# Neighbourhood attention in a fused encoder layer: a deeper pipeline, with the value products of two blocks in one run

## The chip, the cores and the metric

The kernel runs on one core of one Trainium2 chip. The metric is the device time of one execution in microseconds (us); lower is better. A core has five engines with a queue of instructions each, worked off in order: TensorE (PE, matrix products), VectorE (DVE), ScalarE (ACT), GpSimd (POOL) and SyncE (SP, here the issuer of nearly all transfers). They wait for one another through semaphores. Tiles live in SBUF, results of TensorE in PSUM.

## The reference

One layer of a hybrid encoder: 1024 tokens and 16 meta tokens of width 1024, all in float32.

```python
u = _rmsnorm(h, norm_g[l])
z = u @ w_in[l]
gq, gk, gv, r_f, r_b, g_gate, nq, nk, nv, n_gate = jnp.split(z, split_at, axis=-1)
...
s_loc = jnp.einsum('bchd,bicjhd->bhcij', q_r, k_g) * scale
...
s = jnp.concatenate([s_loc.reshape(B, H, W, wh * ww), s_meta], axis=-1)
p = jax.nn.softmax(s.astype(jnp.float32), axis=-1).astype(v.dtype)
...
o_na = o_na * jax.nn.silu(n_gate)
h = h + jnp.concatenate([o_gla, o_na], axis=-1) @ w_out[l]
```

Group B, which the change concerns, is neighbourhood attention on a 16 by 64 grid of tokens: 16 heads of 64, each query sees a window of 8 by 16 tokens and the 16 meta tokens.

## The kernel before, in words

Every dense product is made of three matmuls on a high and a low half (`mm3`, lines 413 to 416). The program has three stretches. **Start**, to about 60 us: x is loaded, split, and multiplied by the projection weights of the first pair of heads. **Neighbourhood attention**, to about 620 us: eight pairs of heads, one after the other. **Linear attention and output projection**, to the end.

The order on all engines is written out by one model of TensorE's time in the program, the class `Sched` (lines 70 to 136). A main generator yields what comes next: `("w", ns)` books TensorE time for the matmuls just issued, `("gap", ns)` lets at least that much time pass and fills it with steps of a second generator, the filler; `("to", x)` runs the filler up to a given amount of its own work; `("need", key)` runs it until a key is set. The filler is the dense work of what comes later: in the second stretch `fill_na` (L1348), which gives `dense_na(p)` (eight blocks of queries, keys and values in the natural layout, tiles `pn_na`) and `dense_gate(p)` (the gate, tiles `pz_na`) in turn. `S.defer(ns, fn)` has a function's instructions issued when the model's time has gone on by ns. So the model decides the order of each engine's queue, and the chip's semaphores decide the times.

For a pair, `attn(p)` (L775) waits until the pair's dense blocks are made. `k_prep` (L685) transposes the keys on TensorE (`kt`, L696) and builds the operands `K1` and `K2` on ACT, DVE and POOL; the queries come in pairs of blocks by `q_prep` (L725). After `ATTN_NS` of filler come nine steps. Step s does this:

- `transposes` (L822) of block s-1: six transposes of its probabilities (`pp<-ident,P`, L829), three for each of the two heads, copied out to `PT` by ACT for head 0 and DVE for head 1 (L833, L835). Each head first calls its normalisation (DVE, L813 to L818) if that has not been issued yet.
- `softmax` (L785) of block s: four score matmuls (`s`, L767 and L768), on DVE the bias, the maximum and its negation (L795, L798), on ACT the exponentials (L801, L802), and the normalisation deferred by `NORM_NS`.
- filler up to a share `PV_AT` of the step's part, then `pv` (L839) of block s-1: six products of values and `PT`, each in two passes, so twelve matmuls (`po`, L848). A stationary operand has 64 columns there, so the two heads fill the two halves of the array's columns. The third chunk of blocks 0 and 7 has only 16 rows (the meta tokens, `kvm`); the others take it from `VM`, which two transfers (`v_load`, L680) fill for each pair. After blocks 3 and 7 DVE multiplies by the gate (L858); after block 7 SP stores the pair's result (L860).
- filler for the rest of the step.

Step 8 holds no scores: the transposes of block 7, `LAST_NS` of filler, the value products of block 7. Only then does the next pair's `attn` start with its keys. PSUM has two banks each for the tags `pp` (transposes, keys), `ps` (scores) and `pd` (dense), one for `po` and one for `pt`; a softmax block keeps its two `P` tiles, of which there are four.

Beside this, in the start: `u_diag` (L374) builds on DVE a diagonal tile of the row scales `rs`, and `u_spread` (L378) multiplies it by ones on TensorE (`rb`, L381) to get the scales along the other axis. And for pairs 2 and 4 `wd_load` and `wd_prep` (L1010, L1017) fetch and split the decay weights, `WD_NS` after the pair's start: POOL clears rows, DVE makes the high part, ACT copies it, DVE subtracts twice.

Of the kernel before, what the change touches and what calls it, by code (L numbers as in the profile page):

```python
# [20 lines left out]
NPAIR = 8  # L21
# [15 lines left out]
LAST_NS = 3438.0  # L37
# [14 lines left out]
START_AT = {'load': {2: 9, 3: 15, 4: 18, 5: 21, 6: 27, 7: 34}, 'split': {2: 15, 3: 19, 4: 25, 5: 28, 6: 41, 7: 48}, 'rows': {0: 10, 1: 12, 2: 18, 3: 21, 4: 23, 5: 29, 6: 45, 7: 53}, 'rstd': {0: 15, 1: 16, 2: 21, 3: 27, 4: 35, 5: 43, 6: 48, 7: 55}, 'evac': {0: 18, 1: 21, 2: 27, 3: 35, 4: 43, 5: 52, 6: 59}, 'diag': {0: 31, 1: 42, 2: 42, 3: 55, 4: 55}, 'spread': {0: 46, 1: 63, 2: 57, 3: 59}}  # L52
BANKS = {2: ("po", 1), 3: ("pp", 2), 4: ("pp", 2), 5: ("pd", 2), 6: ("pd", 2), 7: ("po", 1)}
PUMP_AT = 5
LD_NS = (842.0, 589.0, 1838.0)
# [84 lines left out]
def kernel(  # L140
# [231 lines left out]
    dg = {}  # L372

    def u_diag(b):  # L374
        dg[b] = nap.tile([128, 128], F32, tag="dg", name=f"dg{b}", bufs=3)
        dve.tensor_scalar(dg[b], ident, rs[:, b : b + 1], None, OP.mult)

    def u_spread(b):  # L378

        ps = ps_tile("ps", f"rb{b}", 2)  # L380
        pe.matmul(ps[:, 0:128], ones, dg[b], start=True, stop=True)  # L381
        act.activation(rbc[:, b * 128 : b * 128 + 128], ps[:, 0:128], AF.Copy)
        S.adv(220)
# [154 lines left out]
    def dense_na(p):  # L538
# [50 lines left out]
        def at(pos):  # L589
            for kind, fn in (  # L590
                ("load", x_load), ("split", u_split), ("rows", x_rows), ("rstd", u_rstd),
                ("evac", lambda t: tile_evac(banks.pop(t), t)), ("diag", u_diag), ("spread", u_spread),
            ):
# [10 lines left out]
        for b in range(8):  # L604
# [26 lines left out]
            if p == 0 and b == 7:  # L631
                assert not banks
                for i in range(4):
                    if i:
                        S.defer(LD_NS[i - 1], lambda i=i: u_diag(4 + i))
                    S.defer(LS_NS[i], lambda i=i: u_spread(4 + i))
# [138 lines left out]
    def attn(p):  # L775
        yield ("need", ("nat", p))
        yield from k_prep(p)
        vload = v_load(p)
        yield ("gap", ATTN_NS)
        prev = None  # L780
        po = {}
        f0 = S.fill
        f1 = (p + 1) * (NAT_NS + GATE_NS) + (NAT_NS if p < 7 else GLA_NS - 9000.0)

        def softmax(u):  # L785
            n = span(u)[1]
            off = 144 if u == 0 else 0
            sm = nap.tile([128, 8], F32, tag="sm", name=f"sm{p}{u}", bufs=2)
            Ps, norms = [], []
            Q1["rest"]()  # L790
            for a in range(2):
                ps = qk(p, u, a)
                P = nap.tile([128, 432], F32, tag="P", name=f"P{p}{u}{a}", bufs=4)
                mx = sm[:, 4 + a : 5 + a]
                dve.tensor_tensor_reduce(  # L795
                    P[:, :n], ps[:, :n], wt[2 * p + a][:, off : off + n], 1.0, -3.0e38, OP.add, OP.max, mx
                )
                dve.tensor_scalar(mx, mx, -1.0, None, OP.mult)  # L798
                if n == 416:
                    loc, met = P.rearrange("p (b t) -> p b t", t=BLK)[:, :, 0:128], P[:, 128:144]  # L800
                    act.activation(loc, loc, AF.Exp, bias=mx, accum_out=sm[:, a : a + 1])  # L801
                    act.activation(P[:, 295:416:8], met, AF.Exp, bias=mx, accum_out=sm[:, 2 + a : 3 + a])  # L802
                else:
                    loc = P[:, :n]
                    act.activation(loc, loc, AF.Exp, bias=mx, accum_out=sm[:, a : a + 1])
                Ps.append((P, loc))

            if u % 2 == SILU_STEP:
                run_silu()

            def norm(a):
                s = sm[:, a : a + 1]
                r = sm[:, 6 + a : 7 + a]  # L813
                if n == 416:
                    dve.tensor_tensor(s, s, sm[:, 2 + a : 3 + a], OP.add)
                dve.reciprocal(r, s)
                loc = Ps[a][1]
                dve.tensor_scalar(loc, loc, r, None, OP.mult)  # L818

            return Ps, [S.defer(NORM_NS[0], lambda: norm(0)), S.defer(NORM_NS[1], lambda: norm(1))]  # L820

        def transposes(u, Ps, norm):  # L822
            ch = ((0, 128), (144, 128), (128, 16) if u in (0, 7) else (288, 128))
            PT = []
            for a in range(2):
                norm[a]()
                pp = ps_tile("pp", f"pp{p}{u}{a}", 2)
                for c, (c0, w) in enumerate(ch):
                    pe.transpose(pp[:w, c * 128 : c * 128 + 128], Ps[a][0][:, c0 : c0 + w], ident)  # L829
                t = nap.tile([128, 384], F32, tag="PT", name=f"PT{p}{u}{a}", bufs=4)  # L830
                for w, e0, e1 in ((128, 0, 256), (16, 256, 384)) if u in (0, 7) else ((128, 0, 384),):
                    if a == 0:
                        act.activation(t[:w, e0:e1], pp[:w, e0:e1], AF.Copy)  # L833
                    else:
                        dve.tensor_copy(t[:w, e0:e1], pp[:w, e0:e1])  # L835
                PT.append(t)
            return PT

        def pv(u, PT):  # L839
            u4 = u % 4  # L840
            if u4 == 0:
                po[0] = ps_tile("po", f"po{p}{u}", 1)
            b0 = span(u)[0]
            vals = [vnat[p][:, b0], vnat[p][:, b0 + 1], kvm[p][:, 128:256] if u in (0, 7) else VM[:, b0 + 2]]
            for c, V in enumerate(vals):
                w = V.shape[0]
                for a in range(2):
                    pe.matmul(  # L848
                        po[0][64 * a : 64 * a + 64, u4 * 128 : u4 * 128 + 128],
                        V[:, 64 * a : 64 * a + 64],  # L850
                        PT[a][:w, c * 128 : c * 128 + 128],
                        start=c == 0, stop=c == 2,
                    )
            if u4 == 3:
                finish(gate_rest)
                g = zt[("ng", p)]
                gv = g.rearrange("p (r i c) -> p i r c", r=16, i=8, c=8)[:, u - 3 : u + 1]
                dve.tensor_tensor(gv, po[0].rearrange("p (i r c) -> p i r c", i=4, r=16, c=8), gv, OP.mult)  # L858
                if u == 7:
                    sp.dma_start(o_scr[8 + p], g)  # L860

        for s in range(9):
            PT = None
            if prev is not None:
                PT = transposes(*prev)
                pu = prev[0]
                yield ("w", 654)
            if s < 8:
                prev = (s, *softmax(s))
# [10 lines left out]
            else:  # L880
                yield ("gap", LAST_NS)
            if PT is not None:
# [615 lines left out]
```

## Time and profile before

| | us |
|---|---|
| median of three runs | 1147.07 |
| the three runs | 1146.75, 1147.07, 1149.39 |
| the profiled execution | 1147.51 |
| its span, first to last instruction | 1145.7 |
| PE busy | 1122.2 |
| DVE, ACT, POOL busy | 769.9, 533.5, 300.7 |

The profile is of one execution. Its page gives each engine's busy time, the span in 40 slices, the chain of work that ended last, and groups of equal instructions (line, engine, operation, tile written, tile read, shape, count, busy time, mean duration, idle time before them). The trace behind it gives, for any stretch, the instructions in order of time and what each waited for. Matmuls are pipelined: a duration in the trace covers the whole way through the array, and the next one starts well before it ends, so what a matmul costs is read from the distance between starts.

### The profile page before, as it was taken

How to read it: one execution, taken by the hardware profiler on the slowest of the kernel's cores; microseconds unless marked ns; L12 is line 12 of the kernel's file. 1: busy time of each engine (PE TensorE's matmuls, PEld its weight loads, DVE VectorE, ACT ScalarE, POOL GpSimd, SP SyncE). 2: the span in 40 equal slices, each digit the busy share in tenths (PEclk: the TensorE clock that was granted, in tenths of full speed). 3: DMA queues.
4: the chain of work that ended last, by engine and by line, in shares of the span. 5: the costliest groups of instructions: out<-in, count | busy, mean ns of one | idle time of the engine just before them, and what ended most of it. 6: DMA issues, size and time to landing. Idle time of an engine off the chain costs nothing.

```text
span 1145.7 us, 18925 instructions
## 1 busy us (share of the span) xinstructions
PE 1122.2 (98%) x6739; PEld 976.7 (85%) x6739; DVE 769.9 (67%) x1963; ACT 533.5 (47%) x1379; POOL 300.7 (26%) x415
## 2 busy tenths in 40 slices
PE   8899999999999999999999999999999999999998
PEld 7789898888988889898889789889978978888886
DVE  6867777777677776777665775675486578656352
ACT  6756565664655656565454541542343254313120
POOL 4753535336253443634221101001101000000000
PEclk9999999999999999999999999999999999999999
DMA  8720402203030030401223513512612375314132
GB/s 259 225 75 2 128 2 73 63 2 128 1 109 27 10 120 1 128 2 32 76 57 102 165 28 84 153 36 79 170 42 66 93 206 166 120 42 130 50 115 102
DMA packets 74277, 99.34 MB, mean 87 GB/s; under 512 B 6532, under 2 KB 45188, under 8 KB 74184
## 3 DMA queue, kind: packets, MB, share of 16 engines
q1 hardware_dynamic: 69960, 89.76, 26.0%
q0 software_dynamic: 4224, 8.39, 2.5%
q8 instruction: 53, 0.87, 0.3%
q14 instruction: 40, 0.33, 0.1%
HBM read 72.89 MB, written 21.04 MB: 82 GB/s over the span
## 4 chain that ended last, share of the span: by engine, by line
PE 79%; DVE 7%; issue 5%; POOL 3%; ACT 3%; DMA 2%; SPq 0%; POOLq 0%; DVEq 0%; ACTq 0%
PE pn_na L414 6%; PE pn_na L416 5%; PE pn_na L415 5%; PE pout L414 5%; PE pout L416 5%; PE pout L415 5%; PE po L848 3%; PE pp L829 3%; PE pz_gz L414 3%; PE pz_gz L415 3%; PE pz_gz L416 3%; PE pz_gg L414 2%; PE pn_gv L414 2%; PE pz_gg L416 2%; PE pz_gg L415 2%
## 5 line engine op out<-in xcount | busy, mean ns | idle before, releaser
L414 PE MATMUL pn_na<-wh,uh 128*128 128x384 f32 x512 | 179.7, 351 | 1.5 <-ACT wh L257 1.0
L415 PE MATMUL pn_na<-wl,uh 128*128 128x384 f32 x512 | 173.5, 339 | 1.7 <-POOL wl L258 1.4
L416 PE MATMUL pn_na<-wh,ul 128*128 128x384 f32 x512 | 173.0, 338 | 0.1
L212 POOL TENSOR_SCALAR post<-post 128x1 f32<-128x1 f32 x32 | 6.8, 213 | 378.4 <-ACT on L1219 378.4
L414 PEld LDWEIGHTS pn_na<-wh,uh 128*128 128x128 f32 x512 | 96.4, 188 | 10.0 <-issue 7.8
L414 PE MATMUL pout<-wh,oh 128*128 128x512 f32 x256 | 103.3, 404 | 0.2 <-DVE acc L1343 0.2
L416 PE MATMUL pout<-wh,oh 128*128 128x512 f32 x256 | 101.4, 396 | 0.0
L415 PE MATMUL pout<-wl,oh 128*128 128x512 f32 x256 | 101.4, 396 | 0.0
L415 PEld LDWEIGHTS pn_na<-wl,uh 128*128 128x128 f32 x512 | 96.6, 189 | 4.1 <-POOL wl L258 3.0
L416 PEld LDWEIGHTS pn_na<-wh,ul 128*128 128x128 f32 x512 | 96.4, 188 | 0.8 <-DVE ul L361 0.7
L258 POOL TENSOR_TENSOR wl<-raw,wh 128x512 fp32r<-128x512 f32 (+2 forms) x63 | 83.2, 1337 | 45.0 <-PE pn_gv L415 27.7
L1343 DVE TENSOR_TENSOR acc<-acc,pout 128x512 f32<-128x512 f32 x64 | 43.9, 685 | 66.8 <-PE pout L416 66.8
L801 ACT ACTIVATE P<-P,sm 128x384 f32<-128x384 f32 x96 | 58.4, 609 | 56.2 <-DVE sm L798 56.2
L414 PE MATMUL pn_gv<-wh,uh 128*128 128x256 f32 (+1 forms) x256 | 75.3, 294 | 0.0
L416 PE MATMUL pn_gv<-wh,ul 128*128 128x256 f32 (+1 forms) x256 | 72.8, 285 | 0.0
L415 PE MATMUL pn_gv<-wl,uh 128*128 128x256 f32 (+1 forms) x256 | 72.8, 284 | 0.0
L795 DVE CUSTOM_DVE_ANT_0 P<-s,wt 128x416 f32<-128x416 f32 (+1 forms) x128 | 69.6, 544 | 2.3 <-PE s L768 2.2
L213 POOL TENSOR_TENSOR ss<-ss,epsm 128x4 f32<-128x4 f32 x64 | 69.0, 1078 | 5.3
L818 DVE TENSOR_SCALAR P<-P,sm 128x384 f32<-128x384 f32 (+1 forms) x128 | 66.9, 523 | 4.5
L254 ACT ACTIVATE wh<-raw 128x512 fp32r<-128x512 f32 x63 | 39.5, 630 | 48.7 <-PE pz_gz L415 20.4
L835 DVE COPY PT<-pp 128x384 f32<-128x384 f32 (+1 forms) x80 | 36.3, 470 | 33.5 <-PE pp L829 33.0
L416 PEld LDWEIGHTS pout<-wh,oh 128*128 128x128 f32 x256 | 48.3, 189 | 11.6
(361 smaller groups left out, 2969.4 us busy)
## 6 DMA issues: line engine op xcount, KB each, us to landing
raw<-in_w_na_dram SPq DMA_DIRECT2D x56, 256.0 KB, 2.8
v_scr<-gvst SPq DMA_DIRECT2D x64, 128.0 KB, 2.3
raw<-in_w_o_dram SPq DMA_DIRECT2D x32, 256.0 KB, 3.2
oin<-o_scr SPq DMA_DIRECT2D x32, 256.0 KB, 3.1
v<-v_scr POOLq DMA_DIRECT2D x4, 1536.0 KB, 9.4
VM<-vnat SPq DMA_DIRECT2D x8, 512.0 KB, 4.5
o_scr<-ng SPq DMA_DIRECT2D x8, 512.0 KB, 3.5
raw<-in_w_gz_dram SPq DMA_DIRECT2D x16, 256.0 KB, 2.8
```

The costliest lines, as they stand in the source:

```text
L213: pool.tensor_tensor(dst, dst, epsm[: dst.shape[0], :eng_n], OP.pow)
L254: act.activation(wh[:, :n], r[:, :n], AF.Copy)
L258: pool.tensor_tensor(wl[:, :n], r[:, :n], f32(wh[:, :n]), OP.subtract)
L414: pe.matmul(ps, ah, bh, start=start, stop=False)
L415: pe.matmul(ps, ah, bl, start=False, stop=False)
L416: pe.matmul(ps, al, bh, start=False, stop=stop)
L795: dve.tensor_tensor_reduce(P[:, :n], ps[:, :n], wt[2 * p + a][:, off : off + n], 1.0, -3.0e38, OP.add, OP.max, mx)
L801: act.activation(loc, loc, AF.Exp, bias=mx, accum_out=sm[:, a : a + 1])
L818: dve.tensor_scalar(loc, loc, r, None, OP.mult)
L829: pe.transpose(pp[:w, c * 128 : c * 128 + 128], Ps[a][0][:, c0 : c0 + w], ident)
L835: dve.tensor_copy(t[:w, e0:e1], pp[:w, e0:e1])
L1343: dve.tensor_tensor(a, a, ps, OP.add)
```

## The change

`attn(p)`, called pair by pair, becomes one generator over all pairs, `attn_all`, with two lists: `wait`, the blocks whose softmax is issued, and `done`, those whose transposes are.

```diff
-LAST_NS = 3438.0
+TAIL_NS = (2000.0, 700.0, 800.0)
...
-            sm = nap.tile([128, 8], F32, tag="sm", name=f"sm{p}{u}", bufs=2)
+        sm = nap.tile([128, 8], F32, tag="sm", name=f"sm{p}{u}", bufs=3)
...
-                P = nap.tile([128, 432], F32, tag="P", name=f"P{p}{u}{a}", bufs=4)
+            P = nap.tile([128, 432], F32, tag="P", name=f"P{p}{u}{a}", bufs=6)
...
+    def attn_all():
+        wait, done = [], []
+        def turn():
+            p, u, *rest = wait.pop(0)
+            done.append((p, u, transposes(p, u, *rest)))
+        def gather():
+            while done:
+                pv(*done.pop(0))
+        for p in range(NPAIR + 1):
+            if p < NPAIR:
+                yield ("need", ("nat", p))
+            if wait:
+                turn()
+                yield ("w", 654)
+                yield ("gap", TAIL_NS[0])
+                turn()
+                yield ("w", 654)
+                yield ("gap", TAIL_NS[1])
+            if p < NPAIR:
+                yield from k_prep(p)
+            if done:
+                yield ("gap", TAIL_NS[2])
+                gather()
+                yield ("w", 1420)
+            if p == NPAIR:
+                break
+            vload = v_load(p)
...
+            yield ("gap", ATTN_NS - (TAIL_NS[2] + 1420.0 if p else 0.0))
...
+            for s in range(8):
+                if len(wait) == 2:
+                    turn()
+                    yield ("w", 654)
+                wait.append((p, s, *softmax(p, s)))
                 yield ("w", 460 if s in (0, 7) else 700)
...
-                pv(pu, PT)
-                yield ("w", 710)
+                if s % 2 and s > 1:
+                    if s == 3:
+                        for m in vload:
+                            m()
+                    gather()
+                    yield ("w", 1420)
```

So block u is transposed in step u+2; the value products of blocks 0 and 1, 2 and 3, 4 and 5 stand together in steps 3, 5 and 7; blocks 6 and 7 are transposed one after the other before the next pair's keys, and their products come after those keys are transposed. `softmax`, `transposes` and `pv` are otherwise the same, as are the query preparation and the filler up to `t0` within a step. The calls of `wd_load`, `wd_prep` and `r_static` move from the loop at the end of the program to the place behind `v_load`.

Two further edits. The diagonal tiles go, and the row scales are used as a stationary operand directly:

```diff
-        pe.matmul(ps[:, 0:128], ones, dg[b], start=True, stop=True)
+        pe.matmul(ps[:, 0:128], rs[:, b : b + 1].to_broadcast([128, 128]), ident, start=True, stop=True)
```

with `u_diag`, its eight calls and its places in `START_AT` and `LD_NS` removed. And the decay weights are staged in half the space:

```diff
-        dve.tensor_copy(w[0:98], st[0:98, 0:512])
-        act.activation(st[64:98, 512:1024], f32(w[64:98]), AF.Copy)
-        dve.tensor_tensor(w[64:96], st[64:96, 0:512], st[64:96, 512:1024], OP.subtract)
+        act.activation(w[0:98], st[0:98], AF.Copy)
+        dve.tensor_tensor(w[64:96], st[64:96], f32(w[64:96]), OP.subtract)
```

(the second subtraction reads its two operands from the same new places).

More of the change, by code (lines that the diff above doesn't have):

```diff
@@ new lines, in pv @@
+    def pv(p, u, PT):
+        u4 = u % 4
+        if u4 == 0:
+            po[0] = ps_tile("po", f"po{p}{u}", 1)
+        b0 = span(u)[0]
+        vals = [vnat[p][:, b0], vnat[p][:, b0 + 1], kvm[p][:, 128:256] if u in (0, 7) else VM[:, b0 + 2]]
+        for c, V in enumerate(vals):
+            w = V.shape[0]
+            for a in range(2):
+                pe.matmul(
+                    po[0][64 * a : 64 * a + 64, u4 * 128 : u4 * 128 + 128],
+                    V[:, 64 * a : 64 * a + 64],
+                    PT[a][:w, c * 128 : c * 128 + 128],
+                    start=c == 0, stop=c == 2,
+                )
+        if u4 == 3:
+            finish(gate_rest)
+            g = zt[("ng", p)]
+            gv = g.rearrange("p (r i c) -> p i r c", r=16, i=8, c=8)[:, u - 3 : u + 1]
+            dve.tensor_tensor(gv, po[0].rearrange("p (i r c) -> p i r c", i=4, r=16, c=8), gv, OP.mult)
+            if u == 7:
+                sp.dma_start(o_scr[8 + p], g)
```

176 lines of the change are left out of this document (63 added, 113 removed).

## The prediction

> **What bounds the kernel now.** I read the page first.
>
> ```profile
> PE 1122.2 (98%) x6739; PEld 976.7 (85%) x6739; DVE 769.9 (67%) x1963; ACT 533.5 (47%) x1379; POOL 300.7 (26%) x415
> PE   8899999999999999999999999999999999999998
> PE 79%; DVE 7%; issue 5%; POOL 3%; ACT 3%; DMA 2%; SPq 0%; POOLq 0%; DVEq 0%; ACTq 0%
> ```
>
> TensorE is busy 98% of the span in nearly every slice, and it is four fifths of the chain of waits. Its instructions are in order, so the time is the sum of the distances between its starts: a change pays by what it takes out of that sum, and nothing else counts. The change removes no TensorE product. What it can take out is waiting, and time that is counted busy but is lost between matmuls. The waits first, from the list of who waited for whom, engine PE (us in total, times, longest):
>
> ```profile
> PE pp L829 <- DVE P L818: 3.1, 6, 0.7
> PE rb L381 <- DVE dg L376: 3.1, 2, 2.2
> PE po L848 <- DVE PT L835: 2.2, 2, 1.1
> PE kt L696 <- DVE nat L560: 0.7, 4, 0.2
> ```
>
> These lie where the change works; they sum to 9.1 us. For the time lost inside busy stretches I read TensorE's timeline around value products (start, duration, line, count), and one row of the chain for six transposes that follow them:
>
> ```profile
> 301.67 0.34 PE L415 MATMUL pn_na<-wl,uh 128*128 128x384 f32 x1
> 301.84 0.34 PE L416 MATMUL pn_na<-wh,ul 128*128 128x384 f32 x1
> 302.11 0.66 PE L848 MATMUL po<-PT,vnat 128*64 128x128 f32 x8
> 302.60 0.39 PE L848 MATMUL po<-PT,VM 128*64 128x128 f32 x4
> 302.91 0.44 PE L414 MATMUL pn_na<-wh,uh 128*128 128x384 f32 x1
> 303.19 0.34 PE L415 MATMUL pn_na<-wl,uh 128*128 128x384 f32 x1
> 304.77 0.66 PE pp L829 x6
> ```
>
> **Part 1: half as many runs of value products.** Dense matmuls of 384 columns start 301.84 - 301.67 = 0.17 us apart. Into the run it is 302.11 - 301.84 = 0.27, 0.10 too much; after it, between the first two dense matmuls, 0.28, 0.11 too much. Inside, twelve matmuls go as six pairs, the two heads side by side. Six transposes of the same 128 columns take 0.66, so 0.11 a piece; four pairs take 302.60 - 302.11 = 0.49 against 0.44, and the last two, with the way out, 0.31 against 0.22. So a run costs 0.10 + 0.05 + 0.09 + 0.11 = 0.35 us beyond its work. It comes with entering and leaving, since the four pairs in the middle, with a new value tile between them, show no such loss. A block with the 16-row chunk has one more change:
>
> ```profile
> 335.72 0.66 PE L848 MATMUL po<-PT,vnat 128*64 128x128 f32 x8
> 336.31 0.43 PE L848 MATMUL po<-PT,kvm 16*64 16x128 f32 x4
> 336.67 0.23 PE L690 MATMUL kmt<-ident,kvm 16*128 16x16 f32 x1
> ```
>
> Here the eight take 0.59 to the next start, the four take 0.36: 0.10 + 0.05 = 0.15 more than in the plain run, for the change of rows. A pair of heads had eight runs and will have four. Three of the merges (2 with 3, 4 with 5, 6 with 7, where the 16 rows stand last) save 0.35 each. In the run of blocks 0 and 1 the 16-row chunk stands in the middle, and the way back to 128 rows, which the exit used to hold, is now paid within the run; no row shows it. Its bounds are 0 and a full 0.35; I take the nearest row, the 0.15 of the way there. So 3 x 0.35 + 0.20 = 1.25 a pair, 10.0 us for eight, between 8.4 and 11.2.
>
> The Trainium skill, page "TensorEngine Tiling (Array Packing)", section "Key Properties", says that changing the tiling mode drains the engine; by that rule it is the number of runs that matters, and the trace agrees with 0.35 a run. With the drain of about 128 cycles at 2.4 GHz that the Trainium skill's page "TensorE: Matmul & The Clock Gate" gives in Part 2, two drains would be an estimated 0.11 a run and this part would bring some 3.4 us; the measured starts decide.
>
> **Part 2: transposes two steps behind.** The waits of `pp` for the normalised `P` fall: when block u is transposed, the scores of u+1 lie between. Three of the six are at pairs' ends, where block 7's normalisation stands late on DVE:
>
> ```profile
> 401.34 1.19 DVE P L818
> 402.66 0.52 PE L829 MATMUL pp<-ident,P 128*128 128x128 f32 x3 [0.71 <-DVE P L818]
> ```
>
> Now block 6 comes first there, and block 7 more than 2 us later, by `TAIL_NS`. The two waits of value products for `PT` are those of pairs 2 and 4, and they are the decay weights' doing:
>
> ```profile
> 221.94 0.43 DVE L1021 CAST wd<-wdst 98x512 fp32r<-98x512 f32 x1 [2.05 <-POOL wd L1020]
> 223.06 0.68 DVE L1023 TENSOR_TENSOR wd<-wdst 32x512 fp32r<-32x512 f32 x1 [0.69 <-ACT wdst L1022]
> 223.76 0.75 DVE L1024 SCALAR_TENSOR_TENSOR wd<-wdst,ident 2x512 fp32r<-2x512 f32 x1
> 224.54 0.56 DVE L835 COPY PT<-pp 128x384 f32<-128x384 f32 x1
> 225.15 0.54 PE L848 MATMUL po<-PT,vnat 128*64 128x128 f32 x5 [1.12 <-DVE PT L835]
> ```
>
> DVE stands for POOL and then ACT, and the copy of `PT` is queued behind. After the change this code is deferred from a point after the keys: 20 us on by the model's times is behind the scores of step 3, with the `PT` copies of that step ahead of it on DVE. The wait for POOL is then ACT's, with DVE waiting for ACT, and what is queued behind are the normalisations of block 3, wanted in step 5. I price it at nothing; if that cover fails it costs the old 1.1 again in two pairs. `kt` waited for `nat`, the last key block's scaling; the keys now come after two groups of transposes and 2.7 us of filler, so that wait falls as well. The three kinds are 3.1 + 2.2 + 0.7 = 6.0 us in 12 waits. The view counts idle time from a matmul's modelled end, 0.27 behind its start, where the next would start after 0.11; so each wait cost 0.16 more: 6.0 + 12 x 0.16 = 7.9 us.
>
> **Part 3: the start.** Without the diagonal tiles the 3.1 us of `rb` fall. But see what comes right behind:
>
> ```profile
> 57.90 0.46 PE L381 MATMUL rb<-dg,ones 128*128 128x128 f32 x2 [2.23 <-DVE dg L376]
> L376 DVE TENSOR_SCALAR dg<-ident,rs x8: 270/280/1315, 33.7 to 59.3; 128x128 f32<-128x128 f32 x8
> 60.58 1.48 DVE L560 TENSOR_TENSOR nat<-nat,ss 128x256 f32<-128x256 f32 x1 [1.05 <-POOL ss L213]
> 61.10 1.57 PE L696 MATMUL kt<-ident,nat 128*128 128x128 f32 x8
> 57.90:59.40 1.50, 1.50 (x6) 1.29 (x7) 1.50 (x3) 0.80 (x2) 1.42 (x2) 0.77 0.25 49
> 59.40:62.60 3.20, 3.20 (x15) 2.69 (x14) 1.75 (x3) 0.28 (x1) 3.12 (x4) 0.57 0.45 141
> ```
>
> The last of the eight key transposes needs the last `nat`, done at 62.06, and that one waits for POOL, which the change leaves as it is. TensorE would come to `kt` some 2 to 3 us earlier and wait there. The two rows at the end (a stretch's length, the busy times of PE, PEld, DVE, ACT and POOL, then the granted clock) show another thing: after 2.23 us of idling the clock fell to 0.77 and 0.57 for 4.7 us, partly hidden now by the same wait. Behind the new wait it would be open: 1.50 x 0.23 + 3.20 x 0.43 = 1.7 us. On the other side DVE loses eight small operations ahead of that chain, at most 0.9 us for the three nearest at their median of 0.28. From -0.9 to +1.7; I take 0.
>
> **Part 4: what is added.** At the joint of two pairs, in the old order, TensorE, POOL and DVE:
>
> ```profile
> 123.50 0.82 PE L829 MATMUL pp<-ident,P 128*128 128x128 f32 x6
> 121.43 6.01 POOL L258 TENSOR_TENSOR wl<-raw,wh 128x512 fp32r<-128x512 f32 x4 [0.53 <-ACT wh L257]
> 126.33 1.67 DVE L261 TENSOR_TENSOR wl<-raw,wh 128x512 fp32r<-128x512 f32 x1
> 129.17 1.49 DVE L560 TENSOR_TENSOR nat<-nat,ss 128x256 f32<-128x256 f32 x1 [1.17 <-POOL ss L213]
> 137.33 3.07 DVE L718 SCALAR_TENSOR_TENSOR K<-kt,gk_t,K 64x512 fp32r<-64x512 f32 x4
> 140.18 0.29 PE L767 MATMUL s<-K,Q 128*128 128x272 f32 x1
> ```
>
> `K2` ends at 140.40 with the first scores at 140.18: no slack there, but the time from the keys to the scores stays 7 us, and the gate product that stood ahead of the `K2` operations on DVE is now queued behind them. With it the store of the result moves behind them too, and SP holds the two `VM` loads behind that store:
>
> ```profile
> VM<-vnat SPq DMA_DIRECT2D x8, 512.0 KB, 4.5
> o_scr<-ng SPq DMA_DIRECT2D x8, 512.0 KB, 3.5
> ```
>
> The two loads in sequence are 9 us, and `VM` is wanted only in step 3, two and a half steps of 5 us or more after the first scores: nothing. The tighter places are the `PT` copies of blocks 6 and 7, queued on DVE behind that `nat` and holding the two `pp` banks that the keys want, and the splits `wl` on POOL, which the gate's matmuls now want about 0.6 us earlier since no transposes stand before them. Also the keys start about 3 us later in the filler (model: 4.5 + 2.6 + 1.3 us of filler before them against 3.9), so the eight steps have less dense work between their softmaxes:
>
> ```profile
> 159.20:166.00 6.80, 6.80 (x50) 6.29 (x49) 5.26 (x18) 5.34 (x16) 2.31 (x5) 1.00 0.01 1
> 118.20:140.20 22.00, 21.84 (x130) 18.24 (x129) 17.70 (x37) 11.20 (x25) 15.37 (x16) 1.00 0.54 166
> ```
>
> DVE is busy 5.26 of 6.80 us in a step; the even steps, with no value products, will be near 5.3 us, the odd ones above 7, so a pair of steps still leaves DVE a fifth. New waits: from nothing to the size of the old ones at joints, 0.71 + 0.16 = 0.87 a pair or 7 us. I take a quarter of a us a pair, 2.0, nearer to nothing because the added step of distance is longer than any wait shown.
>
> **Sum.** 10.0 + 7.9 + 0 - 2.0 = 15.9 us less. The profiled execution was 1147.51 (span 1145.7 and 1.8 around it), so 1131.6; it stands 0.4 above the median of 1147.07, so 1131.2 as a median.
>
> **Rivals.** (a) The waits only move: part 1 pays, and what part 2 frees comes back at joints, splits and in DVE's even steps, with the clock at the start open: 10.0 + 7.9 - 7 - 1.7 = 9.2 less, 1137.9. For it: DVE busy 17.70 of 22.00 us at joints; against it: every wait in the list is for work one step old. (b) The merged run does not save: entry and exit recur with each block. Then 7.9 - 2.0 = 5.9 remain, 1141.2. Against it: within a run a new value tile costs nothing. (c) Slower: at each of seven joints DVE stands behind `nat`, which stands for POOL, `PT` of block 6 is copied late, the second `pp` bank stays taken and TensorE idles. In the old times `nat` ends at 130.66 and the `PT` copy behind it (0.56) at 131.2; block 7's second head would want the bank at 123.50 + 4.5 + 0.65 + 2.6 + 0.3 = 131.55 (the dense blocks' end, then the model's times). So it decides once POOL is over 0.3 us later. At 2.2 us, the length that cost the clock at the start, a joint would lose 2.2 + 1.7 = 3.9, seven 27, against 17.9 gained: 9 slower, 1156. For it: POOL's 6 us without a pause; against it: POOL has the same work and more time before the keys. The Trainium skill's clock page (Part 1) says that the clock falls only after an idle window of about 3.4 us, by which such joints would cost 2.2 alone and the result be near 1145; the trace's 2.23 us at the start, with 0.57 behind it, speaks for the dearer price.
>
> **How the numbers follow.** Chances: the forecast 0.65, (a) 0.20, (b) 0.06, (c) 0.05, and 0.04 for more than the sum's upper end. The best corner is 11.2 + 7.9 + 0.9 = 20.0, 1127; the range goes from 1126 to 1140, which takes in (a). What a measurement of this kernel can tell from no change is 0.3%, 3.4 us, so 1143.6 to 1150.5: part of (b) and of (c) at a lesser wait, 0.05; slower 0.04; faster 0.91.
>
> **What would show it.** 32 runs of `po` of 24 matmuls, each with one entry of 0.27 and one exit; in a run with `kvm` in the middle the step back near 0.15; no waits of `pp` for `P`, `po` for `PT` or `kt` for `nat` in the second stretch; `rb` without wait and a longer wait of the first pair's `kt`, with the clock below 1.00 behind it. I would be wrong if runs of 24 showed gaps of 0.1 between blocks, if `pp`, `kt` or dense matmuls after 120 us waited for `PT` or `wl` by more than 0.9 a pair, or if the clock fell at joints.

## The result and the profile after

The changed kernel is slower: 1158.13 us median (1157.42 to 1159.10) against 1147.37 (1146.75 to 1149.39) in the same comparison; 1.0091 of the time before, 95% interval 1.0074 to 1.0109. The profiled execution took 1157.42 us with a span of 1155.3. One of the four executions of run 17, below, the profiled one, took 2790 us with TensorE at less than half speed; it is neither counted nor read.

Busy time, granted clock, and shares of the chain of waits, from the page of the changed kernel:

```profile
PE 1119.8 (97%) x6739; PEld 981.5 (85%) x6739; DVE 780.3 (68%) x1953; ACT 532.0 (46%) x1379; POOL 301.0 (26%) x415
PEclk9999999989999999999999999999999999999999
PE 74%; DVE 10%; ACT 8%; issue 5%; POOL 2%; DMA 1%; SPq 0%; ACTq 0%; POOLq 0%; DVEq 0%
```

TensorE's share of the chain fell from 79% to 74%; DVE and ACT took it. TensorE's waits in the stretch of the attention, 60 to 640 us (us in total, times, longest):

```profile
PE s L758 <- DVE Q L732: 10.5, 6, 3.2
PE pm_na L465 <- DVE Q L732: 8.6, 6, 1.4
PE kt L687 <- DVE nat L553: 1.8, 1, 1.8
```

None of the old waits is left between the pairs; the `kt` here is that of the first pair, at the start. In their place the scores `s` and the meta tokens' matmuls `pm_na` wait 19.1 us, both for the query operands `Q` that DVE makes (L732, the operation of L741 before). From one pair's keys to the next the kernel before took 68.1 to 68.6 us (71.0 and 71.6 in the two pairs with decay weights); now it takes 70.0 to 70.1 (74.0 and 73.5).

First the merged runs. TensorE's timeline of pair 3, blocks 0 and 1, then 2 and 3:

```profile
305.72 0.34 PE L409 MATMUL pn_na<-wh,ul 128*128 128x384 f32 x1
305.99 0.66 PE L832 MATMUL po<-PT,vnat 128*64 128x128 f32 x8
306.57 0.43 PE L832 MATMUL po<-PT,kvm 16*64 16x128 f32 x4
306.94 0.66 PE L832 MATMUL po<-PT,vnat 128*64 128x128 f32 x8
307.43 0.39 PE L832 MATMUL po<-PT,VM 128*64 128x128 f32 x4
307.75 0.44 PE L407 MATMUL pn_na<-wh,uh 128*128 128x384 f32 x1
308.03 0.34 PE L408 MATMUL pn_na<-wl,uh 128*128 128x384 f32 x1
...
318.66 0.34 PE L409 MATMUL pn_na<-wh,ul 128*128 128x384 f32 x1
318.93 0.66 PE L832 MATMUL po<-PT,vnat 128*64 128x128 f32 x8
...
320.67 0.34 PE L408 MATMUL pn_na<-wl,uh 128*128 128x384 f32 x1
```

From the last dense start ahead to the second behind, the plain run takes 320.67 - 318.66 = 2.01 us. A single run took 303.19 - 301.84 = 1.35; two of them hold four dense distances of 0.17 and the merged run two (0.35 together, unrounded), so the merge saves 2 x 1.35 - 2.01 - 0.35 = 0.34, forecast 0.35. The run with `kvm` takes 308.03 - 305.72 = 2.31, where two single ones, one with `kvm`, take 1.50 and 1.35 (so measured in run 12); it saves 0.20, as forecast. The step back to 128 rows costs 306.94 - 306.57 = 0.37 against 0.22.

Now where the time went. The six waits of `pm_na`, pair 3: TensorE, ScalarE and DVE.

```profile
296.21 0.29 PE L465 MATMUL pm_na<-wh,um 128*48 128x256 f32 x1 [1.43 <-DVE Q L732]
```
```profile
293.46 1.05 ACT L643 ACTIVATE sig<-ng 128x1024 f32<-128x1024 f32 x1
294.41 0.76 ACT L725 ACTIVATE Q<-qt 64x256 fp32r<-64x256 f32 x2
```
```profile
295.21 0.86 DVE L732 TENSOR_TENSOR Q<-qt,Q 64x256 fp32r<-64x256 f32 x2 [0.74 <-ACT Q L725]
```

`pm_na` and the transposed queries `qt` share the one bank of the tag `pt`. The keys now come some 3 us later in the filler, so the meta matmuls, which belong to the filler, fall earlier in the steps: they start 5.5 us behind the query transposes of step 1 (290.74), where the kernel before had 10.5 us between them (284.89 and 295.35). So they wait until DVE has read `qt`; DVE waits for ACT's copies, which stand behind the gate's exponential of 1.05 us.

Next the scores of steps 4 and 6, pair 3: DVE and POOL after, and the same product of POOL before, with DVE beside it.

```profile
312.18 2.61 DVE L553 TENSOR_TENSOR nat<-nat,ss 128x256 f32<-128x256 f32 x1 [0.89 <-POOL ss L212]
```
```profile
311.13 1.01 POOL L212 TENSOR_TENSOR ss<-ss,epsm 128x4 f32<-128x4 f32 x1
312.11 2.39 POOL L647 TENSOR_TENSOR ng<-ng,sig 128x1024 f32<-128x1024 f32 x1
```
```profile
304.25 0.87 DVE L741 TENSOR_TENSOR Q<-qt,Q 64x256 fp32r<-64x256 f32 x2
304.51 2.40 POOL L656 TENSOR_TENSOR ng<-ng,sig 128x1024 f32<-128x1024 f32 x1
305.15 0.42 DVE L555 TENSOR_REDUCE ss<-sq 128x4 f32<-128x256 f32 x1
305.61 0.56 DVE L835 COPY PT<-pp 128x384 f32<-128x384 f32 x1
```

The scaling of `nat` takes 0.42 us in the median (about 1.5 beside POOL's splits `wl`, in both kernels); here it takes 2.61 and ends 0.29 after POOL's product. It waits for POOL's `ss`, and the product is the next instruction in POOL's queue, so the end of `ss` lets both go at once. Beside the same product before, a DVE operation with one operand in PSUM, a reduction and a copy out of PSUM took their usual time. All that is queued on DVE behind `nat` comes 2.2 us late, and two steps on the scores wait:

```profile
323.92 0.43 PE L758 MATMUL s<-K,Q 128*128 128x416 f32 x1 [1.05 <-DVE Q L732]
```

The scores of step 4 lose some 0.5 us more, in pieces too short for the list of waits. From the transposes to the third score matmul it is 1.03 us in step 3 and 1.56 in step 4 (two rows of each step, those between left out):

```profile
309.42 0.82 PE L813 MATMUL pp<-ident,P 128*128 128x128 f32 x6
310.45 0.38 PE L758 MATMUL s<-K,Q 128*128 128x416 f32 x1
```
```profile
314.49 0.82 PE L813 MATMUL pp<-ident,P 128*128 128x128 f32 x6
316.05 0.46 PE L758 MATMUL s<-K,Q 128*128 128x416 f32 x1
```

Third, the decay weights, in pairs 2 and 4: DVE, then TensorE, then windows (length; busy of PE, PEld, DVE, ACT, POOL; granted clock).

```profile
235.62 0.68 DVE L1040 TENSOR_TENSOR wd<-wdst,wd 32x512 fp32r<-32x512 f32 x1 [2.87 <-ACT wd L1039]
```
```profile
239.34 0.69 PE L758 MATMUL s<-K,Q 128*128 128x416 f32 x1 [3.19 <-DVE Q L732]
```
```profile
239.30:242.00 2.70, 2.67 (x8) 2.63 (x9) 1.75 (x4) 0.00 (x0) 1.66 (x3) 0.50 0.00 0
242.00:245.00 3.00, 3.00 (x12) 3.00 (x10) 2.97 (x5) 0.11 (x1) 1.88 (x1) 0.51 0.00 0
245.00:248.00 3.00, 3.00 (x22) 2.91 (x21) 2.15 (x10) 2.94 (x12) 0.00 (x0) 1.00 0.00 0
```

DVE stands 2.87 us for ACT's copy of the weights; behind it are two normalisations and `Q`. After 3.19 us of idling TensorE's clock is 0.50 for 5.7 us, which costs another 2.7 x 0.50 + 3.0 x 0.49 = 2.8 us. In pair 4 it is low for 3.4 us, 1.7 us lost.

### The profile page after: what moved, and what is told of

Read it like the earlier page. It is cut to its first block, busy times and chain, and to the rows that moved or that the text cites. A ratio compares the mean times of both kernels' runs of the same rounds, so it can differ in the third digit from the quotient of the medians.

```text
span 1155.3 us, 18847 instructions
## 1 busy us (share of the span) xinstructions
PE 1119.8 (97%) x6739; PEld 981.5 (85%) x6739; DVE 780.3 (68%) x1953; ACT 532.0 (46%) x1379; POOL 301.0 (26%) x415
## 4 chain that ended last, share of the span: by engine, by line
PE 74%; DVE 10%; ACT 8%; issue 5%; POOL 2%; DMA 1%; SPq 0%; ACTq 0%; POOLq 0%; DVEq 0%
PE pout L407 5%; PE pout L409 5%; PE pout L408 5%; PE pn_na L407 4%; PE pn_na L408 4%; PE pn_na L409 4%; ACT P L784 3%; PE pz_gz L407 3%; PE po L832 3%; PE pz_gz L408 3%; PE pz_gz L409 3%; PE pz_na L409 3%; PE pz_na L407 3%; PE pz_na L408 3%; PE pz_gg L407 2%
## 5 line engine op out<-in xcount | busy, mean ns | idle before, releaser
L257 POOL TENSOR_TENSOR wl<-raw,wh 128x512 fp32r<-128x512 f32 (+2 forms) x63 | 83.5, 1348 | 36.7 <-PE pn_gv L408 27.6
L553 DVE TENSOR_TENSOR nat<-nat,ss 128x256 f32<-128x256 f32 x64 | 58.1, 907 | 14.6 <-POOL ss L212 14.4
L758 PE MATMUL s<-K,Q 128*128 128x416 f32 (+1 forms) x128 | 47.9, 379 | 10.9 <-DVE Q L732 10.5
```

Source lines behind the costliest of these rows:

```text
L257: pool.tensor_tensor(wl[:, :n], r[:, :n], f32(wh[:, :n]), OP.subtract)
L553: dve.tensor_tensor(qv, qv, ss[:, :, None].to_broadcast([128, 4, 64]), OP.mult)
L758: pe.matmul(ps[:, :n], q1[:, qs], k1, start=True, stop=False)
```

## The experiments

Theory A, **places**: each new wait comes from one moved instruction and can be taken away alone; the gains add. Theory B, **saturation**: DVE has no room for the deeper order, and waits come back whatever is moved. Both were put to single edits of the changed kernel first. The table gives every run: its ratio to the kernel before in the same comparison, and TensorE's waits from 60 to 640 us without the first pair's `kt`, `pdec` and the splits of the start, which aren't of the steps. The waits and the clock are those of the profiled execution. The kernel before has a median of 1147.4 to 1149.9 us in the different comparisons, so differences of times across them are good to 2 or 3 us. For the changed kernel itself they are 19.1 us, with a clock of 0.994; for the kernel before 6.0 and 0.998.

| run | edit of the changed kernel | us | ratio, 95% interval | waits us | clock |
|---|---|---|---|---|---|
| 1 | meta matmuls after block 3 | 1153.84 | 1.0050 [1.0035, 1.0065] | 18.3 | 0.992 |
| 2 | gate product 3600 ns sooner | 1151.19 | 1.0023 [1.0011, 1.0035] | 16.9 | 0.994 |
| 3 | decay weights on DVE 4000 ns later | 1152.31 | 1.0038 [1.0024, 1.0053] | 15.9 | 1.000 |
| 4 | 1 + 2 + 3 | 1154.86 | 1.0060 [1.0043, 1.0077] | 17.2 | 0.993 |
| 5 | meta after block 4, + 2 + 3 | 1144.48 | 0.9958 [0.9944, 0.9973] | 10.6 | 0.997 |
| 6 | 1 + 3, gate product on DVE | 1139.54 | 0.9915 [0.9901, 0.9930] | 8.8 | 0.998 |
| 7 | 2 + 3 | 1141.35 | 0.9931 [0.9917, 0.9946] | 10.5 | 1.000 |
| 8 | 4, gate product in four pieces | 1154.77 | 1.0045 [1.0028, 1.0062] | 18.3 | 0.994 |
| 9 | gate product on DVE alone | 1150.51 | 1.0007 [0.9996, 1.0019] | 17.0 | 0.998 |
| 10 | kernel before, gate product on DVE | 1153.22 | 1.0034 [1.0024, 1.0044] | 8.8 | 0.999 |
| 11 | 1 + 2 + 3, gate product on DVE | 1143.05 | 0.9940 [0.9920, 0.9960] | 11.2 | 0.998 |
| 12 | 11, single value runs | 1163.80 | 1.0116 [1.0100, 1.0133] | 17.9 | 0.991 |
| 13 | 7, gate's exponential behind the query copies | 1152.67 | 1.0026 [1.0016, 1.0037] | 16.2 | 1.000 |
| 14 | 7, meta matmuls after block 1 | 1156.94 | 1.0045 [1.0023, 1.0067] | 16.6 | 0.994 |
| 15 | 13, gate product on DVE | 1145.87 | 0.9958 [0.9946, 0.9969] | 10.7 | 0.999 |
| 16 | 13, single value runs | 1150.66 | 1.0002 [0.9993, 1.0012] | 10.5 | 1.000 |
| 17 | 6, queries ahead of normalisations on DVE | 1172.66 | 1.0213 [1.0188, 1.0238] | - | - |
| 18 | 15, queries ahead of normalisations on DVE | 1165.76 | 1.0149 [1.0126, 1.0173] | 23.6 | 0.998 |

### Runs 1 to 4: each new wait alone, then all three

```diff
-            if meta and b >= (6 if p == 0 else 2) and (b == 6 or S.pe >= S.pt_free):
+            if meta and b >= (6 if p == 0 else 3) and (b == 6 or S.pe >= S.pt_free):
```

> Changed kernel with the meta tokens' matmuls of the next pair placed one dense block later (after block 3 instead of block 2). Theory A (places): the new waits come from single instructions that the longer joint has moved behind one another, here meta matmuls right behind the query transposes of step 1, with which they share the one pt bank; each can be moved on its own and the gains add. Then the 6 waits of pm_na (8.6 us idle, 9.6 by starts) vanish and the time is near 1148.5. Theory B (saturation): DVE has no room in the shorter even steps; a wait that is taken away comes back at the next place. Then under 4 us are gained, 1154 or more, and the waits of s for Q grow.

```diff
-SIG_NS = (6480.0, 10000.0, 16000.0)
+SIG_NS = (6480.0, 10000.0, 12400.0)
```

> Changed kernel with the gate's POOL product (2.4 us) deferred by 12.4 instead of 16 us, which puts it ahead of the query work of step 3 instead of into step 4, where it stands ahead of DVE's nat scaling (2.62 us there, 0.42 elsewhere). Theory A: the waits of the scores of step 6 for Q in pairs 1, 3, 5, 6 (1.29 each) and those of step 4 for the score banks (0.5 each) vanish, 7.2 us, near 1151. Theory B: DVE is as late as before by its own load; under 2 us, 1156 or more.

```diff
-        dve.tensor_tensor(w[64:96], st[64:96], f32(w[64:96]), OP.subtract)
-        dve.scalar_tensor_tensor(w[96:98], f32(w[96:98]), ident[96:98, 97:98], st[96:98], OP.mult, OP.subtract)
+        def low():
+            dve.tensor_tensor(w[64:96], st[64:96], f32(w[64:96]), OP.subtract)
+            dve.scalar_tensor_tensor(w[96:98], f32(w[96:98]), ident[96:98, 97:98], st[96:98], OP.mult, OP.subtract)
+        S.defer(4000.0, low)
```

> Changed kernel with the two DVE subtractions of the decay weights deferred by another 4 us, so that DVE does not stand 2.87 us for ACT's copy in step 3 of pairs 2 and 4. Theory A: the two waits of the scores of step 4 for Q (3.4 each by starts) shrink by about 2.9 each, and the clock stays at 1.00 behind them (about 2.8 and 1.7 us): 10 us, near 1147.5. Theory B: the waits come back in steps 5 and 6 of these pairs; under 5 us, 1153 or more.

> All three moves together. Theory A: the gains add, 27 us: near 1131, 16 below the kernel before, since the value runs and the old waits are as cheap as forecast. Theory B: under 10 us together, 1148 or more.

Against 1158.1 the single edits gain 4.3, 6.9 and 5.8 us, and together 3.3. Each took its own wait away (the meta waits in run 1, four of the scores' six in run 2, those of 3.2 us and the lost clock in run 3), but in run 1 the scores then wait 17.3 us where they waited 10.5,

```profile
PE s L758 <- DVE Q L732: 17.3, 6, 6.4
```

and the sum fails A: run 4 came in where B had it. B fails in run 2, which kept nearly all of its gain, and in run 3, which kept 5.8 of 10 us. Part of what run 3 gained is not the edit's: in the profiled execution the clock stays at 1.00 at the start too, behind the same 1.81 us of waiting for `kt`, where the changed kernel has it at half for 3.4 us and loses 1.7. What run 4 shows, DVE and POOL in pair 3:

```profile
301.68 2.45 DVE L569 TENSOR_TENSOR kvm<-kvm,kvs 16x128 f32<-16x128 f32 x1 [0.61 <-POOL kvs L212]
```
```profile
301.63 2.36 POOL L647 TENSOR_TENSOR ng<-ng,sig 128x1024 f32<-128x1024 f32 x1
```

The meta tokens' scaling, 0.28 us elsewhere, now stands beside POOL's product in place of `nat`, and costs as much. Hence theory C: a DVE operation with two inputs in SBUF is held while POOL's product runs, and what counts is which operation the product falls on. The Trainium skill, page "SBUF — State Buffer", section "Who interferes with whom", says just that of the two engines (one port pair, held by one of them for a whole instruction, wanted by DVE operations with two SBUF inputs). The trace agrees: 2.61 and 2.45 us beside 2.39 and 2.36, and 0.42 for the reduction with a single input.

Two inputs are not a condition, though. In the changed kernel the normalisation's scaling of `P`, with one input tile and one scalar per partition and a median of 0.36 us at this size, takes 1.20 beside POOL's splits `wl`:

```profile
120.35 1.20 DVE L801 TENSOR_SCALAR P<-P,sm 128x272 f32<-128x272 f32 x1
```
```profile
118.24 4.46 POOL L257 TENSOR_TENSOR wl<-raw,wh 128x512 fp32r<-128x512 f32 x3 [0.18 <-ACT wh L256]
```

These splits hold DVE in both orders. Added up from 60 to 640 us, the DVE operations beside them exceed the median of their kind by some 31 us in the kernel before and 36 in the changed one (where by over 0.3 us), so most of that is not new.

### Runs 5 to 8: testing C

> As the kernel with all three moves, but the meta matmuls after block 4 instead of block 3, so that the scaling of the meta keys on DVE (2.45 us behind POOL's gate product there) comes a step after that product. Theory C (port): what made DVE late, in the changed kernel and with the three moves, is a DVE operation with two SBUF inputs issued while POOL works on the 2.4 us gate product; it stands until POOL is done. Kept apart from it, it takes 0.4, the waits of the scores of step 4 (3.5 each in pairs 1, 3, 5, 6, 2.0 in 2 and 4) go, 18 us: near 1138. Theory B (DVE's own load): they stay or move, above 1150.

```diff
-            S.defer(ns[2], lambda: (pool if gpool[0] is None else dve).tensor_tensor(g, g, e, OP.mult)),
+            S.defer(ns[2], lambda: dve.tensor_tensor(g, g, e, OP.mult)),
```

> Meta one block later, decay weights split, and the gate product computed by DVE instead of POOL, at its old deferral of 16 us: about 1.1 us more DVE work a pair, and no long POOL operation in the steps. Theory C: no DVE operation above 1.2 us in the steps, waits of the scores under 1 us a pair, near 1138. Theory B: DVE with more work is later, above 1157.

> Gate product at 12.4 us and decay weights split, the meta matmuls where the changed kernel has them. Theories A and C: the gains of the two single moves (6.9 and 5.8) add, since neither brings a scaling behind the gate product; what stays is pm_na's 9.6: near 1145. Theory B: under 8 together, 1150 or more.

Run 6 puts 1.2 us more on DVE in every pair and is the fastest kernel of the study, 0.9915, ahead of the kernel before as well: that is against B, which had it above 1157. Its waits, then those of run 7:

```profile
PE s L758 <- DVE Q L732: 5.6, 6, 1.2
PE s L758 <- POOL Q L736: 3.2, 3, 1.3
```
```profile
PE pm_na L465 <- DVE Q L732: 8.6, 6, 1.4
PE s L758 <- DVE Q L732: 1.4, 1, 1.4
...
PE s L758 <- POOL Q L736: 0.5, 1, 0.5
```

Run 5 gained less than C had it: the query transposes now wait 3.7 us for the meta scaling in the two pairs with decay weights, and the scores still wait 6.4 us for `Q`. Run 7 gained 16.8 where its two edits alone gave 12.7, and B had under 8. Run 8 asked whether smaller products let DVE in between:

```diff
+        for i in range(4):
+            cs = slice(256 * i, 256 * i + 256)
+            pool.tensor_tensor(g[:, cs], g[:, cs], e[:, cs], OP.mult)
```

> As the kernel with all three moves, with POOL's gate product in four pieces of 256 columns, about 0.6 us each, at the same place in every queue. Theory C: DVE gets in between the pieces, its meta scaling takes under 1.3 instead of 2.45, the waits of step 4 shrink from 3.5 to about 2, 6 to 9 us less than 1154.9. Theory B: POOL's work is the same and so is DVE's; the same 1155.

The time says no. DVE, then POOL, which works its four pieces off without a pause:

```profile
300.65 2.89 DVE L569 TENSOR_TENSOR kvm<-kvm,kvs 16x128 f32<-16x128 f32 x1 [0.61 <-POOL kvs L212]
```
```profile
300.60 2.79 POOL L647 TENSOR_TENSOR ng<-ng,sig 128x256 f32<-128x256 f32 x4
```

By the Trainium skill's page "SBUF — State Buffer" ("Who interferes with whom") the ports are held for one instruction, so DVE could have come in after one piece of some 0.7 us. In pairs 1, 3, 5 and 6 `kvm` waits out all four instead. In pairs 2 and 4, where `nat` falls on the pieces, it is done after one:

```profile
233.84 0.75 DVE L553 TENSOR_TENSOR nat<-nat,ss 128x256 f32<-128x256 f32 x1
```
```profile
232.88 3.00 POOL L647 TENSOR_TENSOR ng<-ng,sig 128x256 f32<-128x256 f32 x4
```

So pieces can let DVE in, and why `kvm` isn't let in stays open. Whether pieces with pauses between them would help wasn't tried.

### Runs 9 and 10: the product's engine alone, in both orders

> The changed kernel with one edit: the 1024-column gate product runs on VectorE in place of GpSimd, at its place of the changed kernel. Theory C (a VectorE operation with two SBUF inputs waits while GpSimd's 2.4-us product runs): the scaling of nat is back at 0.42 us beside it, the waits of the scores of step 6 go, the six meta waits of 1.4 us and the two of 3.2 us behind the decay weights stay; 1150 to 1154, a gain of 4 to 8 us on 1158.1. Theory B (VectorE has no room left, 1.1 us more of work in a step makes the waits longer): 1158 or more.

> The kernel before with the same edit and nothing of the change, a control. Theory C: in the old order the product runs beside VectorE operations that read PSUM, and nothing is late, so 1148 within 2 us. Rival (the product on GpSimd costs wherever it stands, and the gain of the gate product on VectorE has nothing to do with the change): faster by 4 us or more, 1144 or less. Theory B: slower by 2 us or more.

The same edit gains 7.6 us in the changed kernel, as C had it, and loses 3.7 in the kernel before, where C had nothing, and where `pp` waits 6.6 us for the normalised `P` instead of 3.1:

```profile
PE pp L829 <- DVE P L818: 6.6, 12, 0.7
```

So POOL's product is not slow as such; it is the new place that makes it dear. The old order did have no room for more on DVE, which B claimed of the new one. Over all the traces I added, for the eight gate products, by how much the DVE operations beside them exceed the median of their kind (where over 0.3 us): before 0.0, after 13.8, run 7 5.5, run 13 15.1, and none where DVE does the product.

### Runs 11 to 16: the waits that were left, and the merged runs on the clock

> The changed kernel with four edits: meta matmuls from block 3, third deferral of the gate 12400 ns, gate product on VectorE, the two VectorE subtractions of the decay weights 4000 ns later. Theory C: no VectorE operation above 1.2 us left in the steps, the scores wait less than the 8.8 us that the kernel with the product on VectorE at 16000 ns showed (1139.5); with 2 to 4 us of waits, 1133 to 1137. Theory B: the waits come back elsewhere, 1140 or more.

> The kernel of the four edits, with the value runs of blocks 0 to 5 of a pair alone (each at its own step, as many runs as before the change bar the last of a pair). It prices the merged runs on the clock: by the forecast 0.20 + 0.35 + 0.35 us a pair, 7.2 us over eight pairs, so that much slower than the kernel of the four edits. Rival (a merged run saves nothing on the clock, since TensorE's time is not the bound): within 2 us of it.

```diff
-                if s % 2 and s > 1:
-                    if s == 3:
+                if s > 1:
+                    if s == 2:
                         for m in vload:
                             m()
                     gather()
-                    yield ("w", 1420)
+                    yield ("w", 710)
```

> The changed kernel with the gate's third deferral at 12400 ns, the decay weights 4000 ns later, and the first exponential of the gate (1.05 us on ScalarE) issued behind the two query copies of step 1 instead of ahead of them. If the meta matmuls wait because the query copies stand behind that exponential, the copies start 1.0 us sooner, the six waits of 1.4 us fall to about 0.4, and the time is 6 us under the kernel of the two edits (0.9931 of before): 0.988 of before, 1135. Rival (a wait removed comes back at another place, as it did with four edits): 0.991 or more.

```diff
-        if u % 2 == SILU_STEP:
-            run_silu()
...
                     q_prep(p, s // 2 + 1)
+                    run_silu()
```

> The changed kernel with the same first two edits and the meta matmuls allowed one block sooner, ahead of the query transposes of step 1, so that they do not need the bank behind them. Place theory: the six waits of 1.4 us go (8.6 us), 0.986 of before, unless the transposes of step 1 now wait for the meta scaling, as they did in two pairs with the meta matmuls after block 4 (2.0 us a wait: then 0.990 to 0.995).

> The kernel of the moved exponential, with the gate product on VectorE at step 3, where on GpSimd it stands beside operations that read PSUM. Theory C (only a VectorE operation with two SBUF inputs beside the product pays): nothing is gained here, and 1.2 us more of VectorE work a pair can make the scores late, so equal or up to 4 us slower, as in the kernel before. Rival (the product on GpSimd costs at any place): faster by 2 us or more.

> The kernel of the moved exponential, with the value runs of blocks 0 to 5 of a pair alone. With few waits in either, the difference prices the merged runs: 7.2 us (0.20 + 0.35 + 0.35 a pair). The same edit to the kernel of the four edits cost 20.7 us, of which its lists of waits show 6.7 and the clock (0.991 beside 0.998) some more. If the merged runs are worth more than the forecast had it, 12 us or more without waits.

All six missed the figure that I had written first; in runs 11, 13 and 15 the time of the other theory or rival came. Run 11 kept 11.2 us of waits: the meta scaling now stands on DVE in step 3, in a row with the product. Run 13 cut the meta waits from 8.6 to 5.0 us, but its later exponential moved POOL's product onto `nat` again:

```profile
309.86 2.62 DVE L553 TENSOR_TENSOR nat<-nat,ss 128x256 f32<-128x256 f32 x1 [0.88 <-POOL ss L212]
```
```profile
309.80 2.40 POOL L647 TENSOR_TENSOR ng<-ng,sig 128x1024 f32<-128x1024 f32 x1
```

So run 15 was no test at a harmless place: with the product on DVE it is 6.8 us faster than run 13, which by what I had written speaks for the rival, but the product it replaces stood beside `nat`, and there C wants that gain too; the rival falls by run 10. Run 14 lost its meta waits and has 12.3 us of waits of the scores for POOL's part of the queries instead. In run 16 the product stands beside a sum of 128 by 1 of the normalisation instead, which then takes 1.41 us; nobody wants that sum for two steps. Single value runs there came out 2.0 us faster than merged ones, while in run 12 they were 20.7 slower, with the clock at 0.991. These two do not price the merge, since the edit moves the filler and with it every deferred operation. The price stands in the timelines: in runs 12 and 16 single runs take 1.35 us again, in 11 and 15 merged ones 2.01.

### Runs 17 and 18: DVE's order

```diff
-        Q1["rest"] = S.defer(0 if i == 0 else Q_NS, rest)
+        Q1["rest"] = S.defer(0 if i == 0 else 600.0, rest)
```

> The kernel with the meta matmuls from block 3, the gate product on VectorE at 16000 ns and the later decay weights (0.9915 of before), with one edit more: the VectorE part of the queries is deferred by 600 ns in place of 1420, so that it stands ahead of the two normalisations of its step, which the change wants only two steps later. Places: the nine waits of the scores for the queries (8.8 us) are 1.0 to 1.3 us each, the two normalisations take 1.9 us on VectorE, so all go; 0.984 to 0.987 of before, 1131 to 1135, which is what the sum of the prediction gave without new waits. Saturation: another wait comes in their place, 0.990 or more.

> The kernel of the moved exponential with the gate product on VectorE at 12400 ns (0.9958 of before; 10.5 us of waits for the queries: 5.0 of the meta matmuls, 5.5 of the scores), with the same edit. Places: most of the 10.5 us goes, 0.987 to 0.989 of before. Saturation: 0.994 or more.

Both went the other way, by 33.1 and 19.9 us. DVE's own waits in run 15, then in run 18:

```profile
DVE Q L732 <- ACT Q L725: 31.4, 14, 3.9
```
```profile
DVE Q L732 <- ACT Q L725: 80.7, 31, 3.3
```

The query operation now comes to the head of DVE's queue before ACT has copied its input, and DVE stands idle 49.3 us more, with the normalisations, which could have run, behind it. The scores no longer wait for DVE's part of the queries, but for POOL's part they wait 6.8 us, in run 15 2.0, and waits of other kinds come (`pz_na` for POOL's splits 4.4, `s` for the previous scores' bank 3.3, `po` for `PT` 2.5). A needs more than a place: it needs the order in which inputs become ready. That run 17 has the same cause is argued from the same edit only.

## Why the prediction was wrong

**Part 1** was right in size: 32 runs of 24, 0.34 and 0.20 us saved a merge, the change of rows 0.15. **Part 2** was right: no `pp`, `po` or `kt` waits of the old kind in the pairs. **Part 3** came out near nothing as forecast: `rb` waits 1.1 instead of 3.1, `kt` then 1.8, with the clock open behind it,

```profile
60.60:62.40 1.80, 1.80 (x5) 1.51 (x6) 0.06 (x1) 0.00 (x0) 1.80 (x2) 0.51 0.46 146
```

and the first scores of pair 0 came at 71.8 us, before at 72.1.

**Part 4** is the step that failed: "New waits: from nothing to the size of the old ones at joints, 0.71 + 0.16 = 0.87 a pair or 7 us. I take a quarter of a us a pair, 2.0". The result lies 1158.1 - 1131.2 = 27 us above the forecast, which held 2.0 of this term, so the term should have been 29 us. The profiled execution shows 19.1 us of listed waits; 12 x 0.16 = 1.9 more by the prediction's own correction for modelled ends; by the granted clock of 0.994 beside 0.998, 0.004 x 1155 = 4.6; and some 0.5 in step 4 of four pairs, 2. Together that is 27.6 of the 29.

As a check the other way, take the changed kernels with merged runs and a clock of 0.998 or more: their ratios on 1147.4, less their listed waits, should come to the sum without new waits, 1129.2 (1147.07 - 10.0 - 7.9). Runs 6, 7 and 11 give 1128.8, 1129.0 and 1129.3; runs 9 and 15 give 1131.2 and 1131.9; runs 13, 3 and 18 give 1134, 1136 and 1141. So the listed waits explain the first five to within 3 us, and in the last three 5 to 12 us stay unexplained.

Three things were wrong in that term. It looked at the joints, and no listed wait is there; they are in steps 1, 4 and 6, where I had only counted DVE's share (5.26 of 6.80) and not what stands at the head of its queue. It said that the deeper order only lengthens distances; but shifting the keys by 3 us in the filler moved two pairs of things closer together, neither of which the prediction looked at: the meta matmuls and the query transposes, which share a bank, and the gate product and `nat`, which have no semaphore between them. And of the decay weights it said "I price it at nothing; if that cover fails it costs the old 1.1 again in two pairs": the cover failed, at 3.2 us in two pairs and with the clock behind it. Rival (c) had the right sign and kind (DVE's queue blocked by its head, idling long enough to cost the clock), but its place, the joints, and its engine, POOL late at `ss`, were not it, and that its 1156 lies near the measured 1158 is luck. Rivals (a) and (b) are not what happened either: the old waits did not move, and the merged runs pay. Of (a), the words "DVE's even steps" name the place of the scores' waits, but it priced all new waits at 7 us.

What is settled: that the gate product at its new place holds `nat`, by the traces and by runs 9 and 10; the decay weights and the clock behind them, by run 3; the meta matmuls' bank, by run 1, whose own wait went. Theory B is refuted where it says that more work on DVE must cost time (run 6), but not where it says that a wait taken away comes back elsewhere: that happened in runs 1, 4, 11, 14 and 18. What stays open is whether some order gives all of the 16 us; the best found, run 6, gives 9.7.

## What to carry to other kernels

A deeper pipeline moves each deferred operation against all the others, so list for each one what it newly stands beside, ahead of and behind on its engine, whether a semaphore links them or not. For a queue that is worked off in order, a share of busy time says little; ask which instruction comes to its head before its input is ready. When a single edit gives less than its wait, look for the next operation at the same place before calling the engine full.

## What the runs showed of the hardware

POOL's product of 2.4 us held DVE operations with two inputs in SBUF whatever their size: 0.42 became 2.61, 0.28 became 2.45, and a sum of 128 by 1, which began later, took 1.41. POOL's splits also held an operation with one input tile, which took 1.20 where its median is 0.36. Four pieces in a row held one DVE operation for 2.89 us and let another end after 0.75.

TensorE's clock was at 0.50 to 0.51 after 3.19 us of idling, and also after 1.81 at the start, for some microseconds of work. The Trainium skill, page "TensorE: Matmul & The Clock Gate", Part 1, puts the idle window at about 3.4 us; both were shorter. The length of the idling does not decide alone: in runs 3, 4 and 7 the wait at the start was 1.81 to 1.82 us as well, and the clock behind it stayed at 1.00.
